# Asking for a chain's decay rows and unit matrices two projections earlier, and letting row stores queue behind weight requests

## The chip, the cores and the metric

The kernel runs on one core of a Trainium2 chip. The metric is device microseconds of one execution. The core has a matrix engine (PE), a vector engine (DVE), a scalar engine (ACT), a general engine (POOL) and a sync engine (SP), which here does nothing but issue DMAs. Each engine works through its own instructions in the order in which the program gives them, and waits at an instruction until its semaphores are there.

## The reference, cut to what matters

```python
h = rms_norm(x, attn_norm[l])
proj = einsum("bsd,de->bse", h, w_in[l])              # 4096 rows, 1024 -> 4104 columns
o_a = gated_delta_net(q_a, k_a, v_a, g_a, beta, alpha)  # 4 heads, chunked, triangular solve
o_b = retention(q_b, k_b, v_b, g_b, cos, sin)           # 4 heads, chunked
x = x + einsum("bse,ed->bsd", concat(o_a, o_b), w_out[l])
x = x + hierarchical_moe(rms_norm(x, ffn_norm[l]), ...)
return rms_norm(x, final_norm)

# inside gated_delta_net: gc is the running sum of the log decay in a chunk
diff = gc[..., :, None] - gc[..., None, :]
decay = where(causal, exp(where(causal, diff, 0.0)), 0.0)
a_mat = where(strict, einsum("bhnid,bhnjd->bhnij", kb, k) * decay, 0.0)
uw = triangular_solve(a_mat, rhs, unit_diagonal=True)
q_dec = q * exp(gc)
```

## The kernel before, in words

The first 2,110 us or so, the mixer, go through the sequence in eight blocks of 512 rows (`sb`). In each block four stages follow one another: `a1`, `b1`, `a0`, `b0`. An `a` stage projects a pair of delta-net heads, a `b` stage a pair of retention heads. A stage has four groups of weights, and a group four units; a unit is one projection of 24 matmuls into one of two PSUM buffers `acc`, with everything that the other engines do beside it. In an `a` stage the groups are gate, q, k and v; in a `b` stage q, k, v and gate. The next projection but one can't start before DVE or ACT has emptied its `acc` buffer (in a `b` stage's q and k groups by `rqk` L846 and `rb` L849).

When the projections of an `a` stage are done, a *chain* is started for its head pair (`gdn_pair`): a Python generator whose steps are put, by a table of numbers (`PLAN`), between the projections of the following 32 units, so that the chain of `a1` runs during `b1` and `a0`, and that of `a0` during `b0` and the next block's `a1`. In its first step the chain asks for two tiles `E` (L641; the decay row `gc` of a head, copied to all 128 partitions, 256 KB each, from the small DRAM tensor `gcd`, which L380 writes once a block). `decay(i)` reads them: ACT makes `qd = exp(E)` (L653), DVE turns `E` into differences (L657), ACT takes their exponential (L658), and DVE multiplies the chunk's Gram matrices by it (L702, L704). Some steps later the chain asks for `V` (L686), unit rows from the constants, in which DVE then solves the triangular system (L726 to L732). After that come four chunks of the recurrence; each leaves 128 rows in one of two buffers `mx` (L294), and a store of them to DRAM (`mixed`, L296) is put on the list `stores`. The retention chains use the same two buffers. The two buffers named `E` are used a second time within the chain, for masked copies (L749) that PE reads at L784, long before the chunks.

The weights: in block 0 they are loaded raw (`wr`, L131), split into two parts on ACT and DVE (L149, L150) and kept in DRAM (`wsp`, L152). In blocks 1 to 7 the split parts are read back, four loads of 512 KB for each group (`wq`, L143), asked for in the group's first unit (`W` in `STEPS`) for a time that begins with the second quarter of the next group. There are nine buffers `wq`.

All these DMAs go through SP, which handles them in program order. `unit` first calls `store()`, which issues all stores on the list, and then goes through the actions of the unit: `W` or `S` the weights, `L` a tick of the chain, `E` emptying `acc`.

Of the kernel before, what the change touches and what calls it, by code (L numbers as in the profile page):

```python
# [8 lines left out]
F32 = mybir.dt.float32  # L9
# [8 lines left out]
P = 128  # L18
# [3 lines left out]
NT = T // P  # L22
# [8 lines left out]
B = LEVELS[0]  # L31
NB = P // B
NQ = P // (2 * NB * NT)
# [5 lines left out]
C_ROW = C_ID + P  # L39
# [26 lines left out]
def rows(ap, off, pat):  # L66
    return bass.AP(tensor=ap.tensor, offset=ap.offset + off, ap=pat)
# [6 lines left out]
def mixer(tc, outer, banks, x, attn_norm, w_in, conv_a, a_log, dt_bias, norm_a, norm_b, cst, rope, mixed, clear, w_out, x1, wsp):  # L74


    nc = tc.nc
# [5 lines left out]
    with ExitStack() as ctx:  # L83
        cp, gp, sp = (pool(tc, ctx, n, b, side="right") for n, b in (("c", 1), ("g", 2), ("s", 2)))
# [108 lines left out]
        la, lb = Lane(), Lane()  # L193
        late, bg, stores = [], [], []
# [7 lines left out]
            if bg:  # L202
                bg.pop(0)()

        def store():
            due, stores[:] = stores[:], []
            for f in due:
                f()

# [1 line left out]

        def unit(u, evac, kind):

            store()
            g = gi[0]
            act = dict(L=la.tick, E=evac or (lambda: None), T=later, S=lambda: ahead(4 * g + 5, u, False),
                       W=lambda: ahead(4 * g + 5, u, True), B=behind)
            for o in STEPS[kind]:
                act[o]()
            if u == 3:  # L220
                gi[0] += 1

        def w(k):
            m = 4 * gi[0] + k // 2
# [113 lines left out]
        def decays(ba):  # L338
# [41 lines left out]
            nc.sync.dma_start(gcd, gr)  # L380
            yield gcd

        L = dict(locals())
        with tc.manual_schedule():
            x_load(0)
            nc.sync.dma_start(ident, cst[:, C_ID:C_ID + P])
            nc.sync.dma_start(arow, rows(attn_norm, 0, [[0, P], [1, D]]))
            nc.gpsimd.memset(ex[:, 0:8], -0.5)
            nc.gpsimd.memset(ex[:, 8:16], 0.5)
            for m in range(NWR):  # L390
                fetch(m)
            for r in range(1, min(NXI, NT)):
                x_load(r)
            nc.sync.dma_start(nrow[:, :128], rows(norm_a, 0, [[0, P], [1, 128]]))
            nc.sync.dma_start(nrow[:, 128:640], rows(norm_b, 0, [[0, P], [1, 512]]))
            nc.sync.dma_start(nrow[:, 640:644], rows(a_log, 0, [[0, P], [1, 4]]))
            nc.sync.dma_start(nrow[:, 644:648], rows(dt_bias, 0, [[0, P], [1, 4]]))
            prow = mp.tile([P, T], F32, name="cv", bufs=NCV)[:48, :P]
            nc.sync.dma_start(prow, rows(conv_a, 0, [[P, 48], [1, P]]))
            nc.sync.dma_start(C, cst[:, :C_ID])  # L400
            scale = x_norm(0)
            for t in (halo, Sa, Sb, zt):
                nc.gpsimd.memset(t, 0.0)
            scale()
            x_turn(0)
            for m in range(4):
                split(m)
            scale = x_norm(1)
            split(4)

            def setup(i):

                if i:
                    x_turn(i)
                if i < NT - 1:
                    bg.append(scale if i == 0 else x_norm(i + 1))
                if i == 0:
                    nc.vector.tensor_scalar(nrow[:, :640], nrow[:, :640], 0.5, None, op0=OP.mult)
                    nc.scalar.activation(nega, nrow[:, 640:644], AF.Exp)
                    nc.vector.tensor_scalar(nega, nega, -1.0, None, op0=OP.mult)  # L420
                if i == NT - 1:
                    pp = ptr.tile([P, 512], F32, name="tr")
                    nc.tensor.transpose(pp[:, :48], prow, ident[:48, :48])
                    nc.vector.tensor_copy(pcol, pp[:, :48])
                x_load(i + NXI)

            for sb in range(NS):
                t0 = sb * T
                last = sb == NS - 1
                rt = mp.tile([P, NT, 192], F32, name="rt", bufs=1)  # L430
                nc.sync.dma_start(rt, rows(rope, t0 * 192, [[192, P], [P * 192, NT], [1, 192]]))
                for kind, pr in stages:
                    if (kind, pr) == (("a", 1) if sb else ("a", 0)):
                        for t in clear:
                            zero(nc, t, zt, sb, NS)
                    if kind == "a":

                        n = 264 if pr else 256
                        gs = []
                        if pr:  # L440
                            ba = gp.tile([P, NT, 8], F32, name="ba")
                        for i in range(NT):
                            if pr and not sb:
                                setup(i)
                            if pr and sb and i == 2:
                                next_rows(4 * sb + 3)
                            a = proj_n(i, n)

                            def evac():
                                if pr:  # L450
                                    nc.vector.tensor_copy(ba[:, i], a[:, 256:264])
                                gs.append(silu_gate(a, nrow[:, None, :128].to_broadcast([P, 2, P]), 2))
                            unit(i, evac, "g")
                        if pr:
                            dec = decays(ba)
                            co = next(dec)
                            bg += [lambda: next(dec)] + [lambda: None] * 1 + [lambda: next(dec), lambda: box.append(next(dec))]
                            box = []


                        dst, ready = [], []
                        for wi in range(3):
                            dst.append(gp.tile([P, 2, T], F32, name="qkv"[wi] + "t", bufs=(1, 2, 1)[wi]))
                            for cc in range(2):
                                ch = wi * 4 + 2 * pr + cc
                                a = proj_t(cc)
                                unit(2 * cc + 1, lambda: take(a, ch, dst[wi][:, cc], ready), "t")
                        la.start(gdn_pair(tc, sb, pr, co, box[0], gs, dst, ready, L), PLAN[pr])
                    else:
                        if last and pr and sb:  # L470
                            out.begin()
                        if pr == 0:
                            for r in range(min(NXI, NT)):
                                bg += x_prep(4 * sb + 4 + r)

                        def after(i):
                            next_rows(4 * sb + 4 + i)
                            if last and i < 0:
                                mid.close()
                                out.pool = pool(tc, outer, "mt", 2)  # L480
                            if last and sb and i == 1:
                                out.turn(0)

                        ret_pair(tc, sb, pr, rt, unit, L, after if pr == 0 else None)
            out.second = [hp.tile([P, KC, T], F32R, name=n) for n in ("hh", "hl")]
            todo = list(range(M0 + 5, len(quarters)))

            def splits(n):
                for _ in range(n):
                    if todo:  # L490
                        split(todo.pop(0))

            splits(3)
            n = S // P - NT
            units = iter(())
            if n:
                units = out.units(n - 2)
            while la.chain or lb.chain or late or bg or stores:
                store()
                next(units, None)  # L500
                lb.tick()
                la.tick()
                later()
                splits(2)
                behind()
            splits(len(todo))
            while out.open:
                next(units, None)
# [112 lines left out]
                      zt[:, None, :].to_broadcast([P, m, ZW]))  # L621


def gdn_pair(tc, sb, pr, co, gcd, gs, qkv, ready, L):
    nc = tc.nc
    sp, gp, ptr, psm, ex, Sa = L["sp"], L["gp"], L["ptr"], L["psm"], L["ex"], L["Sa"]
    ident, neg, C, norm_out = L["ident"], L["neg"], L["C"], L["norm_out"]
# [3 lines left out]
    hs = (2 * pr, 2 * pr + 1)  # L631
# [3 lines left out]
    vr = gp.tile([P, 2, NT, P], F32, name="vr", bufs=1)  # L635
    jk = sp.tile([P, P], BF, name="jk", bufs=2)
    tkc = lambda w, i, c: tk[:, w, 4 * i + c:4 * i + c + 1]
    E, qd = [], []
    for i, h in enumerate(hs):
        e = gp.tile([P, NT, P], F32, name="E", bufs=2)  # L640
        nc.sync.dma_start(e, rows(gcd, h * P, [[0, P], [4 * P, NT], [1, P]]))  # L641
        E.append(e)

    def turn(src):
        tr = ptr.tile([P, NT, P], F32, name="tr")
# [36 lines left out]
    blocks = [(slice(b * B, b * B + B), b) for b in range(NB)]  # L682
    at2, N = (gp.tile([P, 2 * NT, P], F32, name=n, bufs=1) for n in ("at", "U"))
    N = N.rearrange("p a b -> p (a b)").rearrange("p (r s) -> p r s", r=B)
    V = sp.tile([P, B // NQ, B], F32, name="V", bufs=1)
    nc.sync.dma_start(V.rearrange("p r s -> p (r s)"), L["cst"][:, C_ROW:])  # L686
    for i, h in enumerate(hs):
        a_ = at2[:, i * NT:i * NT + NT]
        m_ = gp.tile([P, NT, P], F32, name="am")
# [1121 lines left out]
```

## Time and profile before

| | |
|---|---|
| median of 3 runs | 3616.17 us (3609.36 to 3617.98) |
| profiled execution | 3614.18 us, span of its trace 3612.4 us |
| mean granted TensorE clock | 0.978 of full speed |
| PE busy | 94% of the span |
| DVE, ACT, POOL busy | 61%, 42%, 29% |

The span goes from the first to the last instruction of the profiled execution. An engine's busy share counts the time in which one of its instructions ran; waiting, branching and issuing of DMAs are not in it. Times within the trace are microseconds from the start of the span.

### The profile page before, as it was taken

What the parts mean: (1) busy time and instruction counts of PE and PEld (TensorE: products, weight loads), DVE (VectorE), ACT (ScalarE), POOL (GpSimd) and SP (SyncE); (2) the same over time, 40 slices, a digit from 0 to 9 for tenths busy, and PEclk for the clock granted to TensorE, in tenths of its full rate; (3) what the DMA queues carried; (4) which work ended last, traced back from release to release, by engine and by line L of the source; (5) the groups of instructions that cost most, each with busy time, mean ns of one, the idle gap of its engine ahead of it and who ended that gap; (6) DMA issues with size and microseconds to landing.
All of it is one profiled execution on the core that took longest, in us unless ns stands there. A gap on an engine that the chain in (4) does not pass through costs nothing. (4 is left out here: it accounts for less than half of the span.)

```text
span 3612.4 us, 65017 instructions
## 1 busy us (share of the span) xinstructions
PE 3405.1 (94%) x24177; PEld 3118.7 (86%) x24177; DVE 2206.6 (61%) x5766; ACT 1500.5 (42%) x3322; POOL 1052.1 (29%) x1352
## 2 busy tenths in 40 slices
PE   7999999999999999999999999999969999999996
PEld 6988988988998998989899898888858888888885
DVE  6785565575576566466466564444456777777775
ACT  4343233233233333323323332222136666776775
POOL 1322222232232232232222220211223444444443
PEclk9999999999999999999999999999979999999998
DMA  8766346445455355364444435332268898899996
GB/s 269 239 209 216 125 144 208 147 145 189 147 158 191 127 173 187 140 187 162 159 146 172 161 110 168 115 121 97 78 198 287 286 307 291 304 327 331 342 317 194
DMA packets 463375, 711.10 MB, mean 197 GB/s; under 512 B 151329, under 2 KB 342353, under 8 KB 463057
## 3 DMA queue, kind: packets, MB, share of 16 engines
q1 hardware_dynamic: 426688, 622.16, 51.9%
q0 software_dynamic: 34976, 84.20, 6.6%
q8 instruction: 191, 3.13, 0.3%
q14 instruction: 128, 1.04, 0.1%
q10 hardware_dynamic: 1392, 0.56, 0.1%
HBM read 606.32 MB, written 131.99 MB: 204 GB/s over the span
## 5 line engine op out<-in xcount | busy, mean ns | idle before, releaser
L244 PE MATMUL acc<-wq,hh 128*128 128x256 f32 (+1 forms) x2560 | 760.1, 297 | 92.8 <-issue 51.4
L245 PE MATMUL acc<-wq,hh 128*128 128x256 f32 (+1 forms) x2560 | 733.5, 287 | 1.9 <-DVE wq L150 1.9
L246 PE MATMUL acc<-wq,hl 128*128 128x256 f32 (+1 forms) x2560 | 733.0, 286 | 2.1 <-DVE hl L324 2.1
L244 PEld LDWEIGHTS acc<-wq,hh 128*128 128x128 f32 x2560 | 495.6, 194 | 104.4 <-issue 63.9
L245 PEld LDWEIGHTS acc<-wq,hh 128*128 128x128 f32 x2560 | 496.7, 194 | 2.4 <-DVE wq L150 2.4
L246 PEld LDWEIGHTS acc<-wq,hl 128*128 128x128 f32 x2560 | 495.1, 193 | 2.8 <-DVE hl L324 2.8
L232 PE MATMUL acc<-hh,wq 128*128 128x512 f32 x768 | 317.8, 414 | 0.5 <-DMA wq<-wsp 0.3
L234 PE MATMUL acc<-hh,wq 128*128 128x512 f32 x768 | 302.1, 393 | 0.0
L233 PE MATMUL acc<-hl,wq 128*128 128x512 f32 x768 | 300.9, 392 | 0.0
L1622 PEld LDWEIGHTS g<-xT,gu 128*128 128x128 f32 x2048 | 273.3, 193 | 15.0 <-DVE xT L1554 5.4
L1622 PE MATMUL g<-xT,gu 128*128 128x128 f32 (+30 forms) x2048 | 279.0, 295 | 2.7 <-DVE xT L1554 2.7
L1622 PE MATMUL u<-xT,gu 128*128 128x128 f32 (+30 forms) x2048 | 275.9, 293 | 0.0
L1622 PEld LDWEIGHTS u<-xT,gu 128*128 128x128 f32 x2048 | 266.3, 191 | 1.9
L272 DVE SCALAR_TENSOR_TENSOR cv<-xin,pcol,cv 128x512 f32<-128x512 f32 x288 | 216.3, 751 | 73.3 <-ACT cv L270 66.5
L280 POOL TENSOR_TENSOR gs<-gs,nrow 128x256 f32<-128x256 f32 x128 | 97.4, 761 | 512.6 <-DVE gs L279 486.9
L850 POOL TENSOR_TENSOR rqk<-rqk,rb 128x256 f32<-128x256 f32 x128 | 116.1, 908 | 250.8 <-DVE rb L849 178.3
L1597 POOL DMA_INDIRECT out_dram<-xg,mi x100 | 131.8, 1318 | 188.0 <-DVE ss L1593 95.9
L976 PE MATMUL y<-dh,hh 128*128 128x512 f32 (+16 forms) x400 | 164.7, 412 | 20.5 <-ACT ys L1565 12.8
L1565 ACT ACTIVATE ys<-y,mf 128x512 f32<-128x512 f32 (+22 forms) x200 | 133.6, 679 | 114.2 <-PE y L978 95.6
L1568 POOL DMA_INDIRECT xg<-out_dram,mi x97 | 100.3, 1034 | 251.6 <-PE tr L1552 45.3
L234 PEld LDWEIGHTS acc<-hh,wq 128*128 128x128 f32 x768 | 144.2, 188 | 32.9
L289 POOL TENSOR_TENSOR ss<-ss,ex 128x2 f32<-128x2 f32 x128 | 101.7, 795 | 238.3 <-DVE ss L288 205.2
(376 smaller groups left out, 8007.1 us busy)
## 6 DMA issues: line engine op xcount, KB each, us to landing
wq<-wsp SPq DMA_DIRECT2D x420, 512.0 KB
gu<-in_w_gate_dram SPq DMA_DIRECT2D x128, 512.0 KB
gu<-in_w_up_dram SPq DMA_DIRECT2D x128, 512.0 KB
dn<-in_w_down_dram SPq DMA_DIRECT2D x64, 1024.0 KB
xi<-in_x_dram SPq DMA_DIRECT2D x64, 512.0 KB
wsp<-wq SPq DMA_DIRECT2D x60, 512.0 KB
mixed<-mx SPq DMA_DIRECT2D x128, 128.0 KB
out_dram<-zt SPq DMA_DIRECT2D x8, 2048.0 KB
```

Source lines behind the costliest of these rows:

```text
L232: nc.tensor.matmul(a, wh[:, s], hh[:, k, :], start=(k == 0), stop=False)
L233: nc.tensor.matmul(a, wh[:, s], hl[:, k, :], start=False, stop=False)
L234: nc.tensor.matmul(a, wl[:, s], hh[:, k, :], start=False, stop=(k == KC - 1))
L244: nc.tensor.matmul(a[:, :n], hh[:, k, s], wh[:, :n], start=(k == 0), stop=False)
L245: nc.tensor.matmul(a[:, :n], hh[:, k, s], wl[:, :n], start=False, stop=False)
L246: nc.tensor.matmul(a[:, :n], hl[:, k, s], wh[:, :n], start=False, stop=(k == KC - 1))
L272: nc.vector.scalar_tensor_tensor(cv, xin[:, j:j + T], tap(j), cv, op0=OP.mult, op1=OP.add)
L850: nc.gpsimd.tensor_tensor(o.rearrange("p h s d -> p (h s d)"), o.rearrange("p h s d -> p (h s d)"), b.rearrange("p h s d -> p (h s d)"), o ...
L976: nc.tensor.matmul(out, a.hi, b.hi, start=(i == 0), stop=False)
L1565: nc.scalar.activation(self.y[:R, s], y[:R], AF.Copy, scale=self.f[:R, WT, self.n:self.n + 1])
L1597: so = nc.gpsimd.indirect_dma_start(out=orow, out_offset=self.idx(0), in_=self.xg[:self.G], in_offset=None, bounds_check=S - 1, oob_is_err ...
L1622: nc.tensor.matmul(o[:, b, :R], self.w.gu[k // 4][:, k % 4, i * DE + b * P:i * DE + b * P + P], self.xT[:, k, :R], start=(k == 0), stop=(k ...
```

## The change

The two loads of `E` and the load of `V` are taken out of the chain and into a function `preload`, which the `a` stage calls ahead of the first projection of its v group. The chain gets the tiles handed to it. `unit` no longer issues the stores first. In the units 0, 1 and 2 of a group, the stores that were on the list when the unit began go out at the unit's end; in unit 3 they go out at its start. What a unit's own chain tick adds waits for the next unit.

```diff
-        def store():
-            due, stores[:] = stores[:], []
+        def store(n=None):
+            due, stores[:n] = stores[:n], []
             for f in due:
                 f()
...
         def unit(u, evac, kind):

-            store()
+            due = len(stores)
+            if u == 3:
+                store()
             g = gi[0]
...
             for o in STEPS[kind]:
                 act[o]()
             if u == 3:
                 gi[0] += 1
+            else:
+                store(due)
...
+        def preload(pr, gcd):
+
+            E = []
+            for h in (2 * pr, 2 * pr + 1):
+                e = gp.tile([P, NT, P], F32, name="E", bufs=2)
+                nc.sync.dma_start(e, rows(gcd, h * P, [[0, P], [4 * P, NT], [1, P]]))
+                E.append(e)
+            V = sp.tile([P, B // NQ, B], F32, name="V", bufs=1)
+            nc.sync.dma_start(V.rearrange("p r s -> p (r s)"), cst[:, C_ROW:])
+            return E, V
+
...
                             for cc in range(2):
+                                if wi == 2 and cc == 0:
+                                    first = preload(pr, box[0])
                                 ch = wi * 4 + 2 * pr + cc
...
-                        la.start(gdn_pair(tc, sb, pr, co, box[0], gs, dst, ready, L), PLAN[pr])
+                        la.start(gdn_pair(tc, sb, pr, co, first, gs, dst, ready, L), PLAN[pr])
...
-def gdn_pair(tc, sb, pr, co, gcd, gs, qkv, ready, L):
+def gdn_pair(tc, sb, pr, co, first, gs, qkv, ready, L):
...
-    E, qd = [], []
-    for i, h in enumerate(hs):
-        e = gp.tile([P, NT, P], F32, name="E", bufs=2)
-        nc.sync.dma_start(e, rows(gcd, h * P, [[0, P], [4 * P, NT], [1, P]]))
-        E.append(e)
+    (E, V), qd = first, []
...
-    V = sp.tile([P, B // NQ, B], F32, name="V", bufs=1)
-    nc.sync.dma_start(V.rearrange("p r s -> p (r s)"), L["cst"][:, C_ROW:])
```

On PE, DVE, ACT and POOL every instruction keeps its place. Only SP's order changes. On SP, in block 1, from the q group of `a1` to the first group of `b1` (`wq` are weights, `mixed` the row stores, `E` and `V` the chain's tiles), it stands so before:

```order
L296 DMA mixed<-mx 128x256
L143 DMA wq<-wsp 128x1024 x4
L296 DMA mixed<-mx 128x256
L143 DMA wq<-wsp 128x1024 x4
L296 DMA mixed<-mx 128x256 x2
L143 DMA wq<-wsp 128x1024 x4
L641 DMA E<-gcd 128x4x128 x2
L686 DMA V<-in_cst_dram 128x256
```

With the change the same stretch of SP reads:

```order
L143 DMA wq<-wsp 128x1024 x4
L300 DMA mixed<-mx 128x256 x2
L392 DMA E<-gcd 128x4x128 x2
L395 DMA V<-in_cst_dram 128x256
L143 DMA wq<-wsp 128x1024 x4
L300 DMA mixed<-mx 128x256
L143 DMA wq<-wsp 128x1024 x4
L300 DMA mixed<-mx 128x256
```

`E` and `V` stood behind the three weight requests of the k, v and first `b1` group and behind four stores; now they stand behind the k group's weights and two stores, ahead of the v group's weights. Each store stands behind a weight request that it stood ahead of.

In the chain of `a0`, still block 1, SP has before, from the q group of `a0` to the first group of `b0`:

```order
L296 DMA mixed<-mx 128x256
L143 DMA wq<-wsp 128x1024 x4
L296 DMA mixed<-mx 128x256
L143 DMA wq<-wsp 128x1024 x4
L296 DMA mixed<-mx 128x256
L143 DMA wq<-wsp 128x1024 x4
L296 DMA mixed<-mx 128x256 x2
L143 DMA wq<-wsp 128x1024 x4
L641 DMA E<-gcd 128x4x128 x2
L686 DMA V<-in_cst_dram 128x256
```

and with the change:

```order
L300 DMA mixed<-mx 128x256 x2
L143 DMA wq<-wsp 128x1024 x8
L300 DMA mixed<-mx 128x256 x2
L392 DMA E<-gcd 128x4x128 x2
L395 DMA V<-in_cst_dram 128x256
L143 DMA wq<-wsp 128x1024 x4
L300 DMA mixed<-mx 128x256
L143 DMA wq<-wsp 128x1024 x4
L300 DMA mixed<-mx 128x256
```

Here too `E` and `V` move ahead of the weights of the last two groups and of two stores.

## Rows read from the trace of the kernel before

**Rows 1.** Who PE waited for, blocks 1 to 7: us in total, times, longest.

```profile
PE acc L244 <- issue: 51.4, 14, 4.5
PE acc L244 <- DVE gs L279: 21.6, 8, 3.7
PE acc L244 <- DVE rb L849: 8.9, 9, 1.6
...
PE acc L232 <- DMA wq<-wsp: 0.3, 1, 0.3
```

**Rows 2.** Who ACT waited for, the same stretch.

```profile
ACT qd L653 <- DMA E<-gcd: 58.0, 14, 5.0
```

**Rows 3.** Timeline of SP, 470 to 490 us: start, length, instruction.

```profile
473.67 1.83 SPq L143 DMA_DIRECT2D wq<-wsp  x4
475.60 1.03 SPq L641 DMA_DIRECT2D E<-gcd  x2
```

**Rows 4.** Timeline of ACT, 478.7 to 488 us; in brackets the idle time before.

```profile
483.70 0.63 ACT L653 ACTIVATE qd<-E 128x512 f32<-128x512 f32 x1 [4.59 <-DMA E<-gcd]
```

**Rows 5.** Timeline of DVE, 472 to 506 us.

```profile
473.14 0.41 DVE L846 TENSOR_TENSOR rqk<-acc,rt 128x256 f32<-128x256 f32 x1
...
484.37 2.24 DVE L657 SCALAR_TENSOR_TENSOR E<-E,co,cst 128x128 f32<-128x128 f32 x4 [6.13 <-ACT qd L653]
...
488.19 0.48 DVE L849 TENSOR_TENSOR rb<-acc,rt 128x128 f32<-128x128 f32 x2
```

**Rows 6.** Timeline of PE, 482 to 528 us, the starts after a wait.

```profile
488.77 0.36 PE L244 MATMUL acc<-wq,hh 128*128 128x256 f32 x1 [4.12 <-issue]
...
501.82 0.35 PE L244 MATMUL acc<-wq,hh 128*128 128x256 f32 x1 [0.98 <-DVE rb L849]
...
526.53 0.38 PE L244 MATMUL acc<-wq,hh 128*128 128x256 f32 x1 [2.37 <-DVE gs L279]
```

**Rows 7.** All that DVE waited for, 484.4 to 526.5 us.

```profile
DVE E L657 <- ACT qd L653: 6.1, 1, 6.1
DVE U L712 <- ACT X L711: 1.4, 1, 1.4
```

**Rows 8.** Timelines of ACT, PE and DVE, 345 to 378 us.

```profile
355.79 0.63 ACT L653 ACTIVATE qd<-E 128x512 f32<-128x512 f32 x1 [3.65 <-DMA E<-gcd]
...
360.86 0.55 PE L244 MATMUL acc<-wq,hh 128*128 128x256 f32 x1 [3.17 <-issue]
...
376.46 0.42 DVE L846 TENSOR_TENSOR rqk<-acc,rt 128x256 f32<-128x256 f32 x1 [1.60 <-PE acc L246]
```

**Rows 9.** Timeline of SP, 440 to 456 us.

```profile
453.11 1.82 SPq L143 DMA_DIRECT2D wq<-wsp  x4
```

**Rows 10.** Timeline of SP, 310 to 352 us.

```profile
318.35 1.82 SPq L143 DMA_DIRECT2D wq<-wsp  x4
325.65 0.32 SPq L296 DMA_DIRECT2D mixed<-mx  x1
```

**Rows 11.** Timeline of DVE, 334.9 to 336 us.

```profile
335.08 0.60 DVE L294 SCALAR_TENSOR_TENSOR mx<-sm,ss,gs 128x128 f32<-128x128 f32 x2
```

**Rows 12.** Who PE waited for in block 0's chains, 80 to 262 us.

```profile
PE acc L244 <- DVE rb L849: 4.7, 5, 2.2
PE acc L244 <- DVE st L312: 2.3, 2, 1.8
PE acc L245 <- DVE wq L150: 1.6, 1, 1.6
```

**Rows 13.** Stretch table, L150 on DVE: busy (count), PE clock, DMA.

```profile
206.00:260.00 54.00, 7.61 (x11) 0.97 0.58 194
```

**Rows 14.** Stretch table, PE after three waits: busy (count), granted clock, DMA.

```profile
359.80:366.80 7.00, 5.95 (x28) 0.51 0.22 89
489.50:496.50 7.00, 7.00 (x49) 0.76 0.00 0
624.30:631.30 7.00, 6.98 (x59) 1.00 0.10 38
```

## Prediction

> **What bounds the kernel now.** The mixer is bound by PE, which is busy 94% of the span (the table above); a gain must come out of what PE waits for. I read the list of PE's waits first, cut to blocks 1 to 7 [rows 1]. Its largest entry is 51.4 us in 14 waits of at most 4.5 us, put down to "issue", that is, to nothing that the view can name; weights that came late cost 0.3 us in all. Fourteen is the number of chains in these blocks, two a block. ACT's list for the same stretch has a wait that also occurs 14 times: L653 on the load of `E`, 58.0 us [rows 2].
>
> The timelines join the two. In the chain of `a0` in block 1, SP issues four weight loads at 473.67 and the two `E` loads behind them at 475.60 [rows 3]. ACT has nothing left to do at 479.11 and starts at 483.70, 4.59 us later [rows 4]: the data came 8.1 us after the request, with 2 MB of weights ahead of it. DVE, whose next instruction in order is the `E` difference, starts at 484.37, and only behind that and some small work does it empty the `acc` of the retention projection (L849, done at 488.67) [rows 5]. PE needs that buffer and starts at 488.77, having waited 4.12 us [rows 6]. So "issue" is DVE's late L849, and behind it stands the DMA.
>
> **What sets the end of that stretch.** Taking away PE's wait is not the same as gaining it, so I asked what DVE does next. From 484.4 to 526.5 its whole list of waits is the 6.1 us at the start and 1.4 us for ACT [rows 7], the latter within the chain itself. It never waits for PE there, while PE waits for DVE again at 501.82 (0.98 us) and 526.53 (2.37 us) [rows 6]. This stretch is a DVE stream that begins when `E` lands; if it begins 4.59 us earlier, all of it ends 4.59 us earlier, whatever PE does in between. The gain of an `a0` chain is therefore ACT's wait, not PE's.
>
> In the chain of `a1` ACT waited 3.65 us and PE 3.17 us, but further on DVE waits for PE (1.60 us at 376.46) [rows 8]: here PE has the last word. PE gains its 3.17 us and what its clock gives back (below), up to the 3.65 us by which DVE's stream moves and the little that DVE has to spare. I take ACT's wait here too; it lies between the two.
>
> **The change part by part.**
>
> *E and V earlier on SP.* No instruction is added or removed. In the `a0` chain the loads go out where the v group's weights were asked for, at about 453 [rows 9], with the queue carrying nothing that they stand behind but the k group's weights. With the same 8.1 us they are there at about 461, and ACT wants them at 479.11: 18 us of cover. While that cover lasts the wait is 0; gone, it would cost at most what it costs now. In block 0 no chain waits for `E` (14 waits, 16 chains), so nothing is won there. Removed: 58.0 us [rows 2].
>
> *What they are moved past.* The v group's weights are asked for some 3 us later: `E` takes SP 1.03 us [rows 3], `V` I put at twice that. They were asked for at 453.11 [rows 9]; plus 3 and the 8.1 us of a full queue gives 464. They are first read in the second quarter of the first `b0` projection, which is emptied at 473.14 [rows 5] and so runs from about 470 (24 matmuls at the spacing of 59 in 7 us [rows 14] are 2.9 us). Some 6 us to spare; cost 0.
>
> *Stores behind weights.* The weight requests lose a wait for DVE's rows, but weights are not late (0.3 us [rows 1]): gain 0. The stores are 128 KB each and until the last block nobody reads them; what waits for one is the next but one write to its `mx` buffer. In `b1` such a store will go out behind the weights of 318.35 (1.82 us to issue) [rows 10], about 320.2, and with 8.1 us land at 328.3; the buffer is written again at 335.08 [rows 11]. Cover 6.8 us; cost 0.
>
> *Clock.* After a long wait the granted clock drops: of 7-us stretches behind the 14 waits, two have 0.51 of full speed, nine 0.76 and three 1.00, of which one of each is shown [rows 14]. That is 7 × (2 × 0.49 + 9 × 0.24) = 22 us of full-speed work lost. In the `a0` chains PE has to wait for DVE anyway, so the clock gives back nothing; in the `a1` chains it is what lets PE use more than its 3.17 us. No separate term.
>
> **Sum.** 58.0 us from the profiled execution's 3614.18 us: 3556.2 us. Its own bounds: 51.4 us if only PE's waits are won, less some 3 us for new waits of PE on DVE (3566); and 58 us plus 8 of the 22 us of clock (3548). The median of the runs shown is 2.0 us above the profiled execution; I leave that out. About 0.3%, 11 us, can be told from no change.
>
> **Rivals.**
>
> *A: the clock comes back in full (0.08).* If DVE has more to spare than the `a0` stretch shows, PE wins its 51.4 us and the 22 us: 73 us, 3541 us. Against it: PE's waits for DVE at 501.82 and 526.53. The Trainium skill (TensorE: Matmul & The Clock Gate, "What's actually happening") says that the array's clock is halved by default and that activity releases it, so that each wait removed would also remove a slow stretch. The rows on the clock agree for 11 of the 14 waits; three had none.
>
> *B: DVE takes the wait over (0.16).* Block 0 shows chains whose `E` is in time, and there PE waits for DVE for 4.7 + 2.3 + 1.6 = 8.6 us in two chains [rows 12], 4.3 us each, against 51.4 / 14 = 3.7 us each for `E`. If blocks 1 to 7 fell to that, nearly nothing would be won. Against it: in block 0 DVE also splits weights, 7.6 us in the 54 us of one such chain [rows 13], which later blocks don't have, and that is more than the 4.3 us. Half of that wait returning, 14 × 2.15 = 30 us, leaves 28 us: 3586 us. All of it: no change (0.03 of the 0.16).
>
> *C: `E` is still late (0.02).* SP can't reach `E` before the second chunk's row store has its data, at 325.65 in `b1` [rows 10]; it would have to be stuck there until about 18 us later. Then nothing is won: 3614 us.
>
> *D: slower (0.04).* The row stores land too late for the two `mx` buffers, and DVE waits at L294. It begins when a store that goes out at 320.2 isn't there by 335.08, that is, takes 14.9 us instead of 8.1. Each further us costs DVE, and by it PE, one us in each of 14 chains; beyond 58 / 14 = 4.1 us more, 19 us for the store, the kernel is slower: at 21 us some 28 us, 3642. The Trainium skill (DMA: Bandwidth & Descriptors, "Queues, rings and completion order") says that each DMA engine takes a ring's descriptors in their order, which puts the store's data behind the 2 MB of weights; `E` behind the same 2 MB took 8.1 us in the row, and that is counted above.
>
> **Numbers.** Forecast 0.70, A 0.08, B 0.16, C 0.02, D 0.04. The range goes from A's 3541 to B's half, 3586, which leaves out D, C, the whole of B and part of the rest. All of the forecast, A and most of B is faster by over 11 us: 0.91. Within 11 us: C and all of B, 0.05. Slower: 0.04.
>
> **What would show it.** ACT's list no longer has the wait for `E`, and PE's no longer the 14 "issue" waits. PE's waits on L849 grow in the `b0` stages, from about 1 us to some 2, and those on L279 stay near 2.4. DVE's L657 follows L665 at once. SP's `E` goes out some 25 us before ACT reads it. L294 doesn't wait for a store. The forecast is wrong if PE's new waits on DVE in the chains' first 20 us add up to more than about 2 us a chain, if DVE waits at L294, or if PE waits for `wq`.

## The result, and the profile after

| | before | changed |
|---|---|---|
| median of 4 runs | 3612.77 us (3607.86 to 3617.98) | 3551.25 us (3545.84 to 3554.30) |
| profiled execution | 3614.18 us | 3548.43 us |
| mean granted clock | 0.978 | 0.985 |

The ratio is 0.9828, 95% interval 0.9806 to 0.985: some 61 us faster (54 to 70). The forecast was 3556 us, some 5 us above the median. The two profiled executions lie further apart than the medians, by 65.8 us.

Of the page of the kernel before, the busy time of PE; of the page of the changed kernel, the span and the busy times. PE lost 25 us of busy time with the same instructions, at a higher mean clock.

```profile
PE 3405.1 (94%) x24177; PEld 3118.7 (86%) x24177; DVE 2206.6 (61%) x5766; ACT 1500.5 (42%) x3322; POOL 1052.1 (29%) x1352
...
span 3546.6 us, 65034 instructions
PE 3379.9 (95%) x24177; PEld 3096.5 (87%) x24177; DVE 2207.6 (62%) x5766; ACT 1498.5 (42%) x3322; POOL 1050.5 (30%) x1352
```

Whom PE waited for in blocks 1 to 7 of the changed kernel (the view of [rows 1]; L248, L283, L860 and L236 are L244, L279, L849 and L232 of before).

```profile
PE acc L248 <- DVE gs L283: 21.7, 8, 3.7
PE acc L248 <- DVE rb L860: 18.5, 13, 1.6
PE acc L249 <- DVE wq L150: 1.8, 1, 1.8
PE acc L248 <- DVE st L316: 1.6, 6, 0.3
PE acc L248 <- DVE tk L728: 0.9, 1, 0.9
...
PE acc L236 <- DMA wq<-wsp: 0.3, 1, 0.3
```

The 14 "issue" waits are gone, 51.4 us, and ACT's list for the same stretch has no wait for `E` any more. The wait on L860 has doubled, from 8.9 to 18.5 us; the wait on L283 and that for weights are what they were.

The changed kernel's timelines of SP, ACT, DVE and PE around the start of the chain of `a0` in block 1 (the places of [rows 3 to 6] and [rows 9]; L666 and L670 are L653 and L657 of before).

```profile
449.91 0.32 SPq L300 DMA_DIRECT2D mixed<-mx  x1
450.34 0.98 SPq L392 DMA_DIRECT2D E<-gcd  x2
451.37 0.49 SPq L395 DMA_DIRECT2D V<-in_cst_dram  x1
451.96 1.94 SPq L143 DMA_DIRECT2D wq<-wsp  x4
...
476.23 0.62 ACT L666 ACTIVATE qd<-E 128x512 f32<-128x512 f32 x1
...
476.88 2.28 DVE L670 SCALAR_TENSOR_TENSOR E<-E,co,cst 128x128 f32<-128x128 f32 x4 [1.43 <-ACT qd L666]
...
494.31 0.36 PE L248 MATMUL acc<-wq,hh 128*128 128x256 f32 x1 [1.60 <-DVE rb L860]
```

`E` is asked for at 450.34, 26 us before ACT reads it at 476.23 without waiting. DVE follows with 1.43 us of idle time, for ACT's `qd`, where it had 6.13; the prediction had it follow at once. PE's next wait of more than 0.3 us is at 494.31, for the same DVE instruction as at 501.82 before, for 1.60 us instead of 0.98.

### The profile page after: what moved, and what is told of

Its sections match the earlier page's. It is cut to its first block, busy times and chain, and to the rows that moved or that the text cites. A ratio compares the mean times of both kernels' runs of the same rounds, so it can differ in the third digit from the quotient of the medians.

```text
span 3546.6 us, 65034 instructions
## 1 busy us (share of the span) xinstructions
PE 3379.9 (95%) x24177; PEld 3096.5 (87%) x24177; DVE 2207.6 (62%) x5766; ACT 1498.5 (42%) x3322; POOL 1050.5 (30%) x1352
## 5 line engine op out<-in xcount | busy, mean ns | idle before, releaser
L248 PE MATMUL acc<-wq,hh 128*128 128x256 f32 (+1 forms) x2560 | 752.7, 294 | 53.0 <-DVE rb L860 23.1
L248 PEld LDWEIGHTS acc<-wq,hh 128*128 128x128 f32 x2560 | 488.6, 191 | 64.0 <-issue 26.1
L249 PEld LDWEIGHTS acc<-wq,hh 128*128 128x128 f32 x2560 | 489.1, 191 | 2.5 <-DVE wq L150 2.5
L250 PEld LDWEIGHTS acc<-wq,hl 128*128 128x128 f32 x2560 | 487.6, 190 | 2.8 <-DVE hl L328 2.8
L236 PE MATMUL acc<-hh,wq 128*128 128x512 f32 x768 | 317.7, 414 | 0.3 <-DMA wq<-wsp 0.3
```

Of the source, the lines that this page charges most:

```text
L236: nc.tensor.matmul(a, wh[:, s], hh[:, k, :], start=(k == 0), stop=False)
L248: nc.tensor.matmul(a[:, :n], hh[:, k, s], wh[:, :n], start=(k == 0), stop=False)
L249: nc.tensor.matmul(a[:, :n], hh[:, k, s], wl[:, :n], start=False, stop=False)
L250: nc.tensor.matmul(a[:, :n], hl[:, k, s], wh[:, :n], start=False, stop=(k == KC - 1))
```

## The experiments

**The two halves apart.** First the early request alone: the changed kernel with `unit` as before.

```diff
...
-            due = len(stores)
-            if u == 3:
-                store()
+            store()
...
-            else:
-                store(due)
```

> Only the first half of the change: E and V are asked for ahead of the v group, the row stores go out first in a unit as before. Theory (what counts is that E is asked for well before ACT wants it): the whole gain, 58 to 65 us below the kernel before, and no wait of ACT for E. Rival (the stores' new place wins part of it, since a store that waits for DVE holds the weights up): less than 50 us, the rest missing as waits of PE for weights or for DVE.

Measured: 3555.90 us, ratio 0.9848 (0.9832 to 0.9863), no wait of ACT for `E`: 57 us below the kernel before. The first half alone gives nearly all.

Then the stores alone: the kernel before with only `store` and `unit` changed.

> Only the second half: stores behind the weight requests, E and V asked for within the chain as before. In the chain of a0 in block 1 SP then no longer waits for the store at 473.25 before it asks for the weights; the weights go when PE has left the v group, at about 470, and E right behind them. Theory (E's landing time is all): landed by about 478.7 (8.1 us later), just before ACT wants it at 479.1, so the wait shrinks from 4.1 us a chain to between 0 and 1.5, and the time falls by 37 to 58 us. Rival (only the early request matters, the store order is worth nothing, as the prediction had it): within 5 us of the kernel before, ACT's 58 us of waits unchanged.

Measured: 3550.30 us, ratio 0.9833 (0.9819 to 0.9846). This half alone gives all of it too, 63 us, more than the 37 to 58 that the theory had. The first line is SP's store in the kernel before; the others are the timelines of SP and ACT of this kernel, same chain:

```profile
473.25 0.32 SPq L296 DMA_DIRECT2D mixed<-mx  x1
...
462.49 0.32 SPq L300 DMA_DIRECT2D mixed<-mx  x1
462.90 4.75 SPq L143 DMA_DIRECT2D wq<-wsp  x4
467.75 0.92 SPq L645 DMA_DIRECT2D E<-gcd  x2
473.04 0.33 SPq L300 DMA_DIRECT2D mixed<-mx  x1
...
478.80 0.62 ACT L657 ACTIVATE qd<-E 128x512 f32<-128x512 f32 x1
```

Before, SP stood at the store until DVE had the rows at 473.25, and asked for the weights and `E` behind it [rows 3]. Now it asks for the weights from 462.90, over 4.75 us instead of 1.83, in part because it waits for PE to free their buffers, and for `E` at 467.75, 11 us ahead of ACT; only then does it stand at the store. The rival, which was the prediction's own line on the stores, is refuted.

**Other places for the request.** With the stores as before, `E` and `V` asked for where the chain is started:

```diff
-                                if wi == 2 and cc == 0:
-                                    first = preload(pr, box[0])
...
+                        first = preload(pr, box[0])
                         la.start(gdn_pair(tc, sb, pr, co, first, gs, dst, ready, L), PLAN[pr])
```

> Stores as before; E and V are asked for where the chain is started, behind the v group, one projection ahead of its first step instead of two and more. SP gets there behind the third chunk's store, at about 463 in block 1, 16 us ahead of ACT. Theory: full gain, the same as the changed kernel within 5 us. Rival (the two projections more are needed): a wait for E is left and the gain is smaller by it.

Measured: 3553.82 us, ratio 0.984 (0.9825 to 0.9855), no wait for `E`: the two projections more are not needed.

Then behind the store that waits for DVE, but ahead of that unit's weights:

```diff
...
             store()
+            for f, pr, gcd in asked:
+                f.extend(preload(pr, gcd))
+            asked.clear()
             g = gi[0]
...
+                        first = []
+                        asked.append((first, pr, box[0]))
...
```

> The kernel before with E and V asked for in the first unit of the b stage, behind the row stores that wait for DVE and ahead of that unit's four weight loads: in block 1 at about 473.7 instead of 475.6. Theory (E is late because 2 MB of weights lie ahead of it in the queue): it lands some 3 us after its request, at about 477, ahead of ACT at 479.1; the wait is gone and the time is that of the changed kernel within 5 us. Rival (the wait for the store at 473.25 is what makes E late): a wait of some 3 us a chain is left, and the gain is under 25 us.

Measured: 3552.03 us, ratio 0.9836 (0.9821 to 0.9851). SP and ACT in this kernel:

```profile
470.15 0.32 SPq L299 DMA_DIRECT2D mixed<-mx  x1
470.57 1.01 SPq L391 DMA_DIRECT2D E<-gcd  x2
471.64 0.50 SPq L394 DMA_DIRECT2D V<-in_cst_dram  x1
472.23 2.00 SPq L143 DMA_DIRECT2D wq<-wsp  x4
...
475.91 0.62 ACT L665 ACTIVATE qd<-E 128x512 f32<-128x512 f32 x1
```

Here `E` still goes out behind the store, at the last moment, and is there at the latest 5.3 us later, when ACT comes and doesn't wait (5.3 to 5.4 us in the 14 chains of blocks 1 to 7), against 8.1 us behind the weights (7.0 to 8.6). So either of the two things ahead of it, the store's wait or the 2 MB, made it late only together with the other; taking `E` past the weights, or the weights and `E` past the store, is enough. `V` went out earlier in all these kernels too, but no engine waited for it in the kernel before. The view of `E` in the changed kernel, where in blocks 1 to 7 the last weights were asked for 5.7 us or more ahead of it, gives the landing times themselves, as far as the trace has them:

```profile
DMA to landing us min/median/max: 3.7/5.1/7.3
```

The Trainium skill (DMA: Bandwidth & Descriptors, "Queues, rings and completion order") says that a DMA engine consumes a ring's descriptors in ring order; 5.1 us as a median without the weights just ahead and 8.1 us with them agree with it. The changed kernel run once more in the same group:

> The changed kernel once more, to stand beside the others of this group: 58 to 66 us below the kernel before.

Measured: 3551.88 us, ratio 0.9826 (0.9812 to 0.984), 61 us below the kernel before.

**Who sets the pace.** The changed kernel with the chain's Gram matmuls done twice:

```diff
-                nc.tensor.matmul(g[:, 0, j], kt[:, i, s], kt[:, i, s], start=True, stop=True)
-                nc.tensor.matmul(g[:, 1, j], kt[:, i, s], qt[:, i, s], start=True, stop=True)
+                for _ in range(2):
+                    nc.tensor.matmul(g[:, 0, j], kt[:, i, s], kt[:, i, s], start=True, stop=True)
+                    nc.tensor.matmul(g[:, 1, j], kt[:, i, s], qt[:, i, s], start=True, stop=True)
```

> The changed kernel with each of the chain's 16 Gram matmuls done twice into the same place (same result): 16 more of 0.11 us, 1.8 us of PE a chain, 28 us in 16 chains. Theory (from the chain's start on DVE sets the pace, in a0's chain up to the gate group): in a0 chains it vanishes in PE's 1.6 us wait for L860, in a1 chains what exceeds the 1.25 us wait costs, about 0.5 us each: 0 to 8 us above the changed kernel. Rival (PE sets the pace): 20 to 28 us above it.

Measured: 3572.82 us, ratio 0.9895 (0.9879 to 0.9911): 21.6 us above the changed kernel. Taken at its word that is the rival's number, but the expectation had the size of the filler wrong: in the trace each of these matmuls is two instructions (a pair takes 0.22 us), so 32 more a chain, 3.5 us, and 57 us in all. Of the 57 us 35 are hidden. PE's waits in blocks 1 to 7 and DVE's waits in the `a0` stretch of block 1 (484.4 to 527 us):

```profile
PE acc L248 <- DVE gs L283: 20.8, 8, 3.6
...
DVE U L724 <- ACT X L723: 1.4, 1, 1.4
DVE E L670 <- ACT qd L666: 1.4, 1, 1.4
DVE rqk L858 <- PE acc L250: 0.3, 1, 0.3
```

The filler has eaten the 18.5 us of waits on L860 and left those on L283, and DVE in the `a0` stretch waits for PE for 0.3 us although PE had 3.5 us more to do. There DVE sets the pace; in the `a1` chains most of what exceeds their wait is paid. The times from one chain's first read of `E` to the next one's say the same. In blocks 1 to 7 an `a1` chain's stretch takes 124.5 to 124.7 us, against 122.4 to 122.7 in the changed kernel: some 2.1 of its 3.5 us are paid. The `a0` chains' stretches in blocks 1 to 6 take 131.4 to 132.0 us, against 130.9 to 132.5: next to nothing is paid there, some 0.6 us if only the stretches with the full clock behind L283 (130.9 to 131.0) are compared.

**PE's remaining waits.** The changed kernel with `acc` emptied ahead of the chain's tick in gate groups of `b` stages:

```diff
-STEPS = dict(g="WLTBES", h="WLBST", t="WELSTB", r="WEBLTS", v="WSBLET", y="WLETSB")
+STEPS = dict(g="WLTBES", h="WLBST", t="WELSTB", r="WEBLTS", v="WSBLET", y="WELTSB")
```

> The changed kernel with STEPS y as WELTSB: in a gate group of a b stage DVE and ACT empty acc before the chain's tick instead of behind it. Theory (DVE's chain steps stand ahead of L283 and PE waits for that): of PE's 21.7 us in 8 waits on L283 most is gone, and the time falls by 8 to 18 us below the changed kernel, since DVE waits for PE right behind that place. Rival (DVE is behind by then with work of earlier units, so that the order within the unit doesn't matter): within 4 us.

Measured: 3516.60 us, ratio 0.9736 (0.9722 to 0.975): 35 us below the changed kernel, twice what was expected. The waits on L283 are 21.7 us of that, and the slow clock behind four of them (below) some 6; the rest is not taken apart. And the tick tables respread:

```diff
-PLAN = ['12122113121120011111111111111111', '12122012212111111111111111111111']
+PLAN = ['12112123121120011111111111111111', '12112112212111111111111111111111']
```

> The changed kernel with other tick tables: the step with the transpose L723 gets a unit to itself (12112123... for the chain of a0, 12112112... for that of a1; both fall in with the old tables from the eighth unit on). Theory: PE's 18.5 us in 13 waits on L860 shrink to under 8, and the time falls by 5 to 12 us below the changed kernel. Rival (DVE has the same work in the same stretch, the wait comes back one projection later): within 4 us.

Measured: 3536.55 us, ratio 0.9786 (0.9771 to 0.98): 15 us below, a little more than expected. PE's longest waits in blocks 1 to 7, of the kernel with `acc` emptied first:

```profile
PE acc L248 <- DVE rb L860: 18.3, 13, 1.6
```

and of the kernel with the tables respread:

```profile
PE acc L248 <- DVE gs L283: 23.6, 8, 3.7
PE acc L248 <- PE sm L708: 4.6, 14, 0.3
```

Each edit takes away its own wait and leaves the other. Both together:

> The changed kernel with both edits, acc emptied first in gate groups and the respread tick tables. Alone they gave about 35 and 15 us. Theory (two separate waits of PE, on L283 and on L860, in different places): they add, 45 to 52 us below the changed kernel, about 3503. Rival (both are one lag of DVE, of which either edit takes most): 35 to 40 us below.

Measured: 3495.30 us, ratio 0.9676 (0.966 to 0.9693): 56 us below the changed kernel and some 118 below the one before, the fastest of all here. The two are more than added, by 6 us, and more than either side expected. One reason may be that with the tables respread alone the waits on L283 grew by 1.9 us and the clock fell behind seven of the eight; that was not tested. With both edits, but on the kernel before:

> The kernel before (E late, stores first) with the same two edits. Theory (the late E costs a chain ACT's wait, because DVE's stream starts with it, whatever comes later): the gap to the kernel with both edits and early E is again 58 us or a little more, so about 3561 to 3568. Rival (what the early E won was in part DVE's later lag, which these edits now take away): the gap is only PE's own wait or less, 51 us or below, about 3555 or less.

Measured: 3585.83 us, ratio 0.9922 (0.9904 to 0.994). The gap to the kernel with `E` early is 90 us, which neither side expected. PE's longest wait and ACT's wait for `E` in that kernel, its first and last read of `E`, and PE's stretch table for its blocks 1 to 7:

```profile
PE acc L244 <- issue: 62.4, 14, 5.6
...
ACT qd L653 <- DMA E<-gcd: 56.4, 14, 5.2
...
L653 ACT ACTIVATE qd<-E x32: 612/619/632, 90.4 to 2038.4; 128x512 f32<-128x512 f32 x32
...
262.00:2080.00 1818.00, 1754.22 (x13036) 0.98 0.49 165
```

About the same stretch of work, and the reads of `E`, of the kernel with both edits and `E` early:

```profile
L666 ACT ACTIVATE qd<-E x32: 612/618/622, 86.7 to 1953.4; 128x512 f32<-128x512 f32 x32
...
262.00:2000.00 1738.00, 1732.88 (x13071) 1.00 0.53 173
```

ACT waits for `E` as long as before, but no later wait of PE on DVE is left to soak up what PE wins. The stretch is 80 us shorter: PE is idle for 59 us less (63.8 to 5.1) and busy for 21 us less (1754.22 to 1732.88), at a granted clock of 1.00 instead of 0.98. From the first to the last read of `E` it is 81.3 us (1948.0 to 1866.7), of which ACT's waits are 56.4; the other 24.9 lie in the stretches between the waits. Read together with the 61 us of the kernels without the edits: the price of the late `E` is ACT's wait only while DVE is the slower of the two.

## Why the prediction was right

*What holds PE up.* As read: "issue" was DVE's late L849 behind the late `E`. In every run in which `E` was there in time, the 14 waits are gone.

*The size.* Between the first chain's first read of `E` and the last chain's last one lie 15 chains; in the trace of before (first line) and of the changed kernel (second):

```profile
L653 ACT ACTIVATE qd<-E x32: 612/618/632, 86.8 to 2068.4; 128x512 f32<-128x512 f32 x32
...
L666 ACT ACTIVATE qd<-E x32: 613/617/621, 90.3 to 2004.7; 128x512 f32<-128x512 f32 x32
```

That is 1981.6 and 1914.4 us, a gain of 67.2 where the sum had 58.0. The profiled execution gained 65.8, since this one came to its first chain 3.5 us later and won 2.1 us behind the last one's read; the traces of the other kernels come to the first chain between 86.7 and 91.1 us, late or early `E` alike, so I don't take that for an effect of the change. By the medians, 61 us (54 to 70), the sum is short by some 3 us, which is within the interval; what follows is the difference of these two executions, 9.2 us.

Taken from each chain's read of `E` to the moment at which ACT wants the next chain's `E`, 7.3 of the 9.2 us lie in the `a0` chains' stretches and 1.8 in those of `a1`. What the sum had too small in the `a0` stretches is its term for the clock, which stood at nothing. It looked at the clock behind the `E` waits alone. Behind PE's wait on L279, before, and L283, changed, the clock also moved; the first row of before is that of block 1, and the three of the changed kernel are blocks 1 to 3:

```profile
526.40:530.40 4.00, 3.87 (x20) 0.59 0.12 49
...
519.50:523.50 4.00, 3.94 (x21) 0.60 0.07 27
774.50:778.50 4.00, 3.94 (x34) 1.00 0.03 13
1027.50:1031.50 4.00, 3.92 (x23) 0.67 0.07 28
```

Before, all 8 such waits had a stretch at 1.2 GHz behind them, 0.57 to 0.72 of full speed over 4 us; in the changed kernel 4 of 8, though the waits are as long. What is missing to 1.00, summed over the first seven such stretches and times 4 us, is 2.53 × 4 = 10.1 us before and 1.12 × 4 = 4.5 us in the changed kernel: 5.6 of the 7.3 us. The times of the stretches agree: in blocks 1 to 6 of the changed kernel those with the full clock behind L283 take 130.9 to 131.0 us, the others 132.0 to 132.5, and before, where none had it, they take 131.9 to 133.3. Which of the eight waits has the slow clock behind it differs from execution to execution (last section), so this part of the gain is no fixed term.

*DVE sets the pace in the `a0` chains, and the gain is ACT's wait.* Right there: the doubled Gram matmuls vanish in it.

*In the `a1` chains PE has the last word.* The number came out, the reason did not. In the `a1` chains of blocks 1 to 7 PE waited on L849 in three of seven; on L860 it now waits in all seven, 1.2 to 1.3 us each. Up to that point DVE has the last word there also. The prediction took DVE's wait of 1.60 us for PE as its sign, but that wait is found with `E` early too, and some 3 us ahead of it PE waits for DVE. PE and DVE in the `a1` chain of block 2, before and changed:

```profile
635.97 0.36 PE L244 MATMUL acc<-wq,hh 128*128 128x256 f32 x1 [1.52 <-DVE rb L849]
...
639.09 0.42 DVE L846 TENSOR_TENSOR rqk<-acc,rt 128x256 f32<-128x256 f32 x1 [1.62 <-PE acc L246]
...
625.35 0.36 PE L248 MATMUL acc<-wq,hh 128*128 128x256 f32 x1 [1.32 <-DVE rb L860]
...
628.48 0.42 DVE L857 TENSOR_TENSOR rqk<-acc,rt 128x256 f32<-128x256 f32 x1 [1.62 <-PE acc L250]
```

The chain that the prediction read, that of block 1, is the odd one: its clock stood at 0.51 behind the wait [rows 8, 14], and there the gain was ACT's 3.66 us and 0.9 more. In blocks 2 to 7 it was ACT's wait and 0.0 to 0.2 us, whether the clock behind the wait had been at 1.00 (two chains) or at 0.76 (four). To take ACT's wait for the `a1` chains too was a choice between two values, and it was lucky in that the reason given for it does not hold.

*`E` moved past the weights: cost 0.* Right; the wait for weights is 0.3 us as before. *Stores behind weights: no `mx` wait.* Right in the chains; one wait of 1.9 us for a store stands at 2072 us, behind the last chain's start.

*Stores behind weights: gain 0.* Right as a share of this change, wrong in its reason. The line asked only whether weights were late, and not what else stood behind the store on SP: `E` did, with the weights ahead of it. Alone that half is worth 63 us; on top of the early request it is worth some 4 us (3555.90 to 3551.88), which the intervals do not tell from nothing. The two halves are two ways to the same gain, and don't add.

*Rivals.* Of A, the clock did come back (PE's busy time fell by 25 us), but the time did not with it, since PE then waited more for L860. With both later edits something of A's kind is seen: there the late `E` costs 90 us. B happened in part: the wait on L860 grew by 9.6 us, 0.7 a chain, and the doubled Gram matmuls, which fill the waits on L860, show that it is real slack of PE. In `b0` that wait is 1.6 us, where the prediction had some 2. C and D did not happen.

## What to carry to other kernels

When a small load is late, list everything ahead of it on its queue, with the waits of each: bulk data and a store that waits for an engine can each be harmless, and make it late together. A chain's start that waits for data costs what the slower engine's stream is moved by, so ask of each stretch which engine that is. One wait of DVE for PE does not show that PE sets the pace: look whether PE itself waited for DVE just before. After the slower engine is relieved, the same late load costs more, here 90 us instead of 61. Then look at the next wait, and at what stands ahead of the instruction that ends it: here one letter moved in a step table was worth over half of what the change gave.

## What the runs showed of the hardware

Behind PE's waits of 2.3 to 3.7 us on L279 or L283 the granted clock fell to 1.2 GHz in 8 of 8 cases in the trace of before and in 4 of 8 in that of the changed kernel, so a wait's length alone does not decide it. In the traces of the repeat, of the two halves and of the two other places of the request, all with `E` in time, it was 4, 6, 3, 4 and 4 of 8. Behind the changed kernel's waits of 1.5 to 1.6 us on L860, in the `a0` chains of blocks 1 to 6, it stayed at 2.4 GHz (1.00 of full speed over the 4 us behind each). Why it was all 8 before, in the one trace there is, stays open.
